# A hybrid decoder layer on one core: where the gate weights are loaded, and which tiles hold a sum of the first stage

## Chip, core and metric

The kernel runs on one core of a Trainium2 chip. The metric is the device time of one execution in microseconds (us), median of several runs.

## The reference

One decoder layer over 1024 tokens of width 1024, in float32. A pre-norm feeds one projection whose columns go to two mixers that run side by side; their outputs are concatenated, projected, added to the input and normed.

```python
xn = rms_norm(h, norm_in_g)
proj = jnp.einsum('btd,de->bte', xn, w_in).astype(f32)
q, k, v, g_ret, x_lru, g_lru = jnp.split(proj, IN_SPLITS, axis=-1)
...
o_ret = group_norm_heads(chunkwise_retention(q, k, v)).reshape(B, T, RET_WIDTH)
y_ret = o_ret * jax.nn.silu(g_ret)
xc = causal_depthwise_conv(x_lru, conv_w.astype(f32), conv_b.astype(f32))
o_lru = rg_lru(xc, gate_a_w.astype(f32), gate_a_b.astype(f32), gate_x_w.astype(f32),
               gate_x_b.astype(f32), lru_lambda.astype(f32))
y_lru = o_lru * jax.nn.silu(g_lru)
mixed = jnp.concatenate([y_ret, y_lru], axis=-1).astype(x.dtype)
h = h + jnp.einsum('bte,ed->btd', mixed, w_out)
return rms_norm(h, norm_out_g)
```

Inside `rg_lru` two block-diagonal products with sigmoids (the gates: 8 blocks of 128x128, two weights each) decide the decay of a linear scan.

## The kernel before

Every operand of a large product is split into a high part (a cast to fp32r on ScalarE, L106) and a low part (the rest, by a subtraction on VectorE, L107); a product is then three matmuls, high by high, high by low and low by high (`mm3`, L112), each of 128x128 weights by 512 columns. Products of two-by-two blocks are made with seven products instead of eight (P1 to P7), from sums and differences of the blocks; the parts of the left sums (of the input x, transposed) are kept for the whole projection.

Stages in the order of time. `v_phase` (L249) computes the column block of v and leaves the left parts behind in their pools sP1 to sP7. Its blocks of x are A11, A12, A21, A22, its blocks of weights b11, b12, b21, b22, and its left sums s1 = A21 - A22, s3 = A11 - A21 (written over A21), s2 = s1 - A11 (written over A11), s4 = A12 + s2. Its products run P1, P2, P5, P6, P7, P3, P4, twelve matmuls for each of four token tiles. The weight blocks and the token tiles whose squares give the norm (`token_rms`, L196, ScalarE L201) share the pool "vb" of six tiles of 4 KB a partition, the outputs have the pool "vo" of ten tiles of 2 KB. Late in the stage b21 is loaded once more for P4.

Then `Runner` (L490) goes through quads of 256 columns: for each of four pairs of blocks one quad of x_lru, one of g_lru, one of g_ret, then eight of q and k. In a quad's step it runs that quad's products with the preparation of the next quad's weights between them (`prep1` to `prep4`; sums t24 and t13 in the pool "sums" of two tiles), and after each product takes one closure from the list `fillers`: this is how the convolution, the gates, the scan and the silu gates of quads done before are put between. After the step of a quad of x_lru, `post_x` (L633) appends fifteen closures: three for the convolution of the first block, `gate_w_parts` (L627), which loads the gate weights of the pair and splits them, and the rest, among them `lru_gates` (L583) for each block. These all work in the pool "w4" of ten tiles of 4 KB ("big", L537); the split gate weights have one tile ("gwp"). After that come retention, whose pieces are fillers in the first half of the output projection, and the rest of the output projection with the norm.

The order of an engine's instructions is set by Tile's scheduler at compile time, which hands out the tiles of a pool and may take an instruction ahead of its place in the program. All loads and stores but one are issued by SP, in its queue's order. In the trace a tile of "sums" is named t, ones or graw, a left sum in its pool xA or xS, and the weight blocks bt.

Of the kernel before, what the change touches and what calls it, by code (L numbers as in the profile page):

```python
# [10 lines left out]
F32 = mybir.dt.float32  # L11
# [3 lines left out]
ALU = mybir.AluOpType  # L15

P = 128
# [23 lines left out]
def hybrid_layer(  # L41
# [17 lines left out]
    pe, act, dve, pool, sp = nc.tensor, nc.scalar, nc.vector, nc.gpsimd, nc.sync  # L59
# [7 lines left out]
    def pool_on(side, name, bufs):  # L67
        return tc.tile_pool(name=name, bufs=bufs, side=side, reuse_waits="tile")
# [36 lines left out]
    def split(src, hi, lo):  # L105
        act.copy(out=hi, in_=src)  # L106
        dve.tensor_tensor(out=lo, in0=src, in1=hi.bitcast(F32), op=ALU.subtract)  # L107
# [57 lines left out]
    sums = s_stack.enter_context(pool_on("right", "sums", 2))  # L165


    xs, xr = {}, {}
# [17 lines left out]
    def combine(out, a, b, op):  # L186
        for o, x_, y_ in zip(out, a, b):
            dve.tensor_tensor(out=o, in0=x_, in1=y_, op=op)  # L188

    def x_parts(name, src):  # L190
        xs[name] = Parts(xs_pool[name])
        for i in range(2):
            xs[name].put(i, src[i])
# [53 lines left out]


    def v_phase():  # L249
        with pool_on("left", "vb", 6) as vb, pool_on("left", "vo", 10) as vo:  # L250
            bw, c, todo = {}, {}, []

            def half():
# [13 lines left out]
            def w_parts(name, src):  # L267
                bw[name] = Parts(slabs)
                for i in range(2):
                    bw[name].put(i, src[i])  # L270
# [48 lines left out]
            s1 = [xs_pool["P3"].tile([P, 2, 512], F32, name="xS1", tag="w") for _ in range(2)]  # L319
# [11 lines left out]

            combine(b11, b11, b22, ALU.add)
            w_parts("P6", b11)
            s3 = xr["A21"]
            combine(s3, xr["A11"], s3, ALU.subtract)
            s2 = xr["A11"]
            combine(s2, s1, s2, ALU.subtract)
            x_parts("P6", s2)
            sp.dma_start(out=cst_sb, in_=cst)
            sp.dma_start(out=ident, in_=ident_in)  # L340
            todo.extend(token_rms(vb, "bt"))
# [36 lines left out]
            decay_exponent()  # L378

    v_phase()  # L380


# [154 lines left out]
    def big(dt=F32, name="big"):  # L537
        return w4.tile([P, T], dt, name=name, tag="w4")


    def post_gr(p):
        def gate(h, c):
            dve.tensor_tensor(out=c, in0=c, in1=rstd_b, op=ALU.mult)
            act.activation(out=c, in_=c, func=AF.Silu)
            sp.dma_start(out=g_d[h // 4, :, :, h % 4].rearrange("n p c -> p n c"),
                         in_=c.rearrange("p (n c) -> p n c", n=NT))

        def post(q):
            for i, c in enumerate((q.cx, q.cy)):
                fillers.append(lambda i=i, c=c: gate(2 * p + i, c))  # L550
        return post
# [4 lines left out]
    def lru_conv(b, c):  # L556

        cw = [col(PAR_CW + 3 * b + j, b) for j in range(CONV)]

        def tap(d):  # L560
            dve.scalar_tensor_tensor(out=xc[:, d:], in0=c[:, :T - d], scalar=cw[3 - d],  # L561
                                     in1=xc[:, d:], op0=ALU.mult, op1=ALU.add)

        def first():
            nonlocal xc
            dve.tensor_tensor(out=c, in0=c, in1=rstd_b, op=ALU.mult)
            xc = big(name="xc")
            act.activation(out=xc, in_=c, func=AF.Identity, scale=cw[3], bias=col(PAR_CB, b))
            tap(1)

        def rest():
            tap(2)
            tap(3)

        def parts():
            xh, xl = big(F32R, "xh"), big(F32R, "xlo")
            split(xc, xh, xl)
            lru[b] = xc, xh, xl

        xc = None  # L580
        return [first, rest, parts]

    def lru_gates(gw, b):  # L583
        xc, xh, xl = lru[b]
        r, y = big(name="r"), big(name="y")
        o = (b % 2) * 256
        for dst, w, bias in ((r, o, PAR_BA), (y, o + P, PAR_BX)):
            for th in range(2):
                s = slice(th * 512, (th + 1) * 512)
                ps = psum()  # L590
                mm3(ps, tuple(gw[:, i, w:w + P] for i in range(2)), (xh[:, s], xl[:, s]), True, True)
                act.activation(out=dst[:, s], in_=ps, func=AF.Sigmoid, bias=col(bias, b))
        dve.tensor_tensor(out=y, in0=y, in1=xc, op=ALU.mult)
        lru[b] = r, y

    def lru_decay(bs):

        for b in bs:
            r, y = lru[b]
            a = big(name="a")  # L600
            act.activation(out=a, in_=r, func=AF.Exp, scale=c1[:, b:b + 1])
            act.activation(out=r, in_=r, func=AF.Exp, scale=c2[:, b:b + 1])
            act.activation(out=r, in_=r, func=AF.Relu, scale=-1.0, bias=1.0)
            lru[b] = r, y, a

    def lru_root(bs):
        for b in bs:
            act.activation(out=lru[b][0], in_=lru[b][0], func=AF.Sqrt)

    def lru_scan(b):  # L610

        r, y, a = lru[b]
        dve.tensor_tensor(out=y, in0=y, in1=r, op=ALU.mult)
        dve.tensor_tensor_scan(out=y, data0=a, data1=y, initial=0.0, op0=ALU.mult, op1=ALU.add)  # L614

    def lru_gated(b, g):
        y = lru.pop(b)[1]
        dve.tensor_tensor(out=y, in0=y, in1=g[b], op=ALU.mult)
        sp.dma_start(out=l_d[b], in_=y)

    def lru_quads():
        quads = []
        for p in range(4):
            bs = (2 * p, 2 * p + 1)
            g, gw = {}, []

            def gate_w_parts(p=p, gw=gw):  # L627
                gr = sums.tile([P, 2, 512], F32, name="graw", tag="sum")
                sp.dma_start(out=gr[:, 0], in_=gate_w[:, 512 * p:512 * p + 512])
                gw.append(gwp.tile([P, 2, 512], F32R, name="gw", tag="gw"))  # L630
                split(gr[:, 0], gw[0][:, 0], gw[0][:, 1])

            def post_x(q, bs=bs, gw=gw, gate_w_parts=gate_w_parts):  # L633
                x0, x1 = lru_conv(bs[0], q.cx), lru_conv(bs[1], q.cy)
                fillers.extend(x0 + [
                    gate_w_parts, x1[0], lambda: lru_gates(gw[0], bs[0]), *x1[1:], None, None,
                    lambda: lru_gates(gw[0], bs[1]), lambda: lru_decay(bs), lambda: lru_root(bs), lambda: lru_scan(bs[0]),
                    lambda: lru_scan(bs[1])])

            def post_g(q, bs=bs, g=g):  # L640
                def gate(b, c):
                    dve.tensor_tensor(out=c, in0=c, in1=rstd_b, op=ALU.mult)
                    act.activation(out=c, in_=c, func=AF.Silu)
                    g[b] = c
                for b, c in zip(bs, (q.cx, q.cy)):
                    fillers.extend([lambda b=b, c=c: gate(b, c), lambda b=b: lru_gated(b, g)])

            quads.append(Quad(C_XL + 256 * p, w4, "w4", post_x))
            quads.append(Quad(C_GL + 256 * p, w4, "w4", post_g))
            quads.append(Quad(C_G + 256 * p, w4, "w4", post_gr(p)))  # L650
        return quads
# [497 lines left out]
```

## Time and profile before

| | us |
|---|---|
| median of 3 runs (748.37 to 748.61) | 748.6 |
| the profiled execution | 748.8 |
| its span, first to last instruction | 747.0 |
| TensorE busy (PE) | 724.4 |
| VectorE busy (DVE) | 582.7 |
| ScalarE busy (ACT) | 425.5 |

Times in the views are microseconds from the start of the span. In a timeline row stand the start, the duration, the engine, the line of the code, the operation, what it writes and reads, the count of like instructions merged into the row, and in brackets the idle time of the engine before it with what ended it. SPq and PEld are SP's queue of transfers and TensorE's loading of weights. The ends of matmuls are modelled and overlap; their starts are what counts.

### The profile page before, as it was taken

The page shows a single profiled execution, that of the slowest core. Times are in us where ns is not written, and L with a number is a line of the kernel's source. Part 1 is how long each engine was busy: PE and PEld are TensorE (multiplying, and loading weights), DVE is VectorE, ACT ScalarE, POOL GpSimd, SP SyncE. Part 2 cuts the span into 40 slices and gives each one's busy share as a digit, 9 for nine tenths or more (in the row PEclk, how much of TensorE's full clock was granted, in tenths as well). Part 3 has the DMA queues.
Part 4 walks back from the last instruction along what each step waited for, and adds up shares of the span by engine and source line. Part 5 has one row for each costly group of instructions (what it writes and reads, how often), then busy time and mean ns, then how long its engine had stood idle before and what let it go on. Part 6 is the DMA issues. An engine that isn't in the chain of part 4 may idle for free.

```text
span 747.0 us, 9358 instructions
## 1 busy us (share of the span) xinstructions
PE 724.4 (97%) x3448; PEld 601.7 (81%) x3448; DVE 582.7 (78%) x960; ACT 425.5 (57%) x649; POOL 0.2 (0%) x4
## 2 busy tenths in 40 slices
PE   6999999999999999999999999997999999999995
PEld 5877888887788788878788888886989988888884
DVE  6899647678977977996799988686467565779996
ACT  6795435695689679669833333244444445424545
POOL 0000000000000000000000000000000000000000
PEclk9999999999999999999999999999899999999998
DMA  9862712122213410421644444569897776272006
GB/s 308 279 207 86 254 56 72 57 84 85 70 57 105 135 57 32 142 97 54 197 126 128 114 113 113 141 187 286 273 312 255 253 210 211 72 228 81 1 0 226
DMA packets 93806, 107.68 MB, mean 144 GB/s; under 512 B 4928, under 2 KB 66752, under 8 KB 93760
## 3 DMA queue, kind: packets, MB, share of 16 engines
q1 hardware_dynamic: 93616, 106.82, 45.5%
q8 instruction: 27, 0.44, 0.2%
q10 hardware_dynamic: 144, 0.26, 0.1%
q14 instruction: 19, 0.16, 0.1%
HBM read 77.71 MB, written 29.36 MB: 143 GB/s over the span
## 4 chain that ended last, share of the span: by engine, by line
PE 55%; DVE 22%; ACT 11%; DMA 7%; issue 4%; SPq 0%; DVEq 0%; ACTq 0%
PE pp L112 47%; DVE xc L561 2%; DVE h L1003 2%; PE pp L796 2%; PE pp L835 2%; PE pp L834 2%; DVE wt L107 2%; PE pp L817 1%; DVE wq L107 1%; DVE y L614 1%; PE pp L856 1%; ACT wq L106 1%; DVE blk L188 1%; DMA rot<-in_rot_t 1%; DMA blk<-o_d 1%
## 5 line engine op out<-in xcount | busy, mean ns | idle before, releaser
L112 PE MATMUL pp<-wh,wq 128*128 128x512 f32 x960 | 301.5, 390 | 1.6 <-DVE cy L471 0.7
L112 PEld LDWEIGHTS pp<-wh,wq 128*128 128x128 f32 x960 | 179.9, 188 | 42.5 <-ACT cy L461 2.3
L112 PE MATMUL pp<-wl,wq 128*128 128x512 f32 x480 | 186.9, 389 | 0.0
L112 PEld LDWEIGHTS pp<-wl,wq 128*128 128x128 f32 x480 | 90.1, 188 | 18.6
L112 PE MATMUL pp<-wo,yt 128*128 128x512 f32 x384 | 98.4, 403 | 0.0
L112 PEld LDWEIGHTS pp<-wo,yt 128*128 128x128 f32 x384 | 70.7, 191 | 13.1
L107 DVE TENSOR_TENSOR wq<-t,wq 128x1024 fp32r<-128x1024 f32 x40 | 48.6, 1220 | 38.6 <-ACT wq L106 31.5
L106 ACT CAST wq<-t 128x1024 fp32r<-128x1024 f32 x40 | 41.7, 1051 | 31.7 <-PE pp L112 22.0
L112 PE MATMUL pp<-wh,w 128*128 128x512 f32 x160 | 52.9, 391 | 0.1
L112 PE MATMUL pp<-wh 128*128 128x512 f32 x112 | 45.5, 406 | 6.9 <-ACT wh L106 6.9
L112 PE MATMUL pp<-wl,wh 128*128 128x512 f32 x112 | 44.6, 400 | 0.0
L112 PE MATMUL pp<-wh,wl 128*128 128x512 f32 x112 | 44.2, 399 | 0.0
L112 PEld LDWEIGHTS pp<-wh,w 128*128 128x128 f32 x160 | 30.0, 188 | 6.9 <-DVE w L107 0.6
L461 ACT COPY cy<-pp 128x512 f32<-128x512 f32 x20 | 11.6, 581 | 41.9 <-PE pp L112 41.3
L848 ACT ACTIVATE yn<-pp,nb,rs_y 128x128 f32<-128x128 f32 x64 | 24.1, 457 | 17.2 <-DVE nb L846 17.2
L112 PEld LDWEIGHTS pp<-wh 128*128 128x128 f32 x112 | 21.7, 194 | 12.1 <-ACT wh L106 7.3
L112 PE MATMUL pp<-wl,w 128*128 128x512 f32 x80 | 31.1, 389 | 0.0
L112 PE MATMUL pp<-wt,ylh 128*128 128x512 f32 x96 | 29.6, 389 | 0.0
L112 PE MATMUL pp<-wt,qkch 128*128 128x512 f32 x96 | 29.6, 389 | 0.0
L422 ACT CAST wq<-wraw 128x512 fp32r<-128x512 f32 x40 | 22.9, 617 | 9.0 <-PE pp L112 8.2
L106 ACT CAST wt<-blk 128x1024 fp32r<-128x1024 f32 x14 | 14.6, 1050 | 21.5 <-PE pp L112 18.0
L424 DVE TENSOR_TENSOR wq<-wraw,wq 128x512 fp32r<-128x512 f32 x40 | 26.8, 681 | 0.1
(179 smaller groups left out, 1303.7 us busy)
## 6 DMA issues: line engine op xcount, KB each, us to landing
wraw<-in_w_in SPq DMA_DIRECT2D x40, 512.0 KB, 4.8
qkc<-qk_d SPq DMA_DIRECT2D x16, 512.0 KB, 6.3
blk<-in_w_out SPq DMA_DIRECT2D x12, 512.0 KB, 5.5
bt<-in_w_in SPq DMA_DIRECT2D x20, 256.0 KB, 5.4
xA<-in_xT SPq DMA_DIRECT2D x16, 256.0 KB, 5.4
v_d<-vo SPq DMA_DIRECT2D x16, 256.0 KB, 2.3
xt<-in_x SPq DMA_DIRECT2D x8, 512.0 KB, 3.3
l_d<-y SPq DMA_DIRECT2D x8, 512.0 KB, 3.0
```

The costliest lines, as they stand in the source:

```text
L106: act.copy(out=hi, in_=src)
L107: dve.tensor_tensor(out=lo, in0=src, in1=hi.bitcast(F32), op=ALU.subtract)
L112: pe.matmul(ps, a, b, start=first and j == 0, stop=last and j == 2, skip_group_check=True)
L422: act.copy(out=h[:, j], in_=b)
L424: dve.tensor_tensor(out=l[:, j], in0=b, in1=h[:, j].bitcast(F32), op=ALU.subtract)
L461: act.copy(out=self.cy[:, :TH], in_=self.A)
L561: dve.scalar_tensor_tensor(out=xc[:, d:], in0=c[:, :T - d], scalar=cw[3 - d], in1=xc[:, d:], op0=ALU.mult, op1=ALU.add)
L796: heads(lambda h, hs: pe.matmul(psc[:, hs], k[:, hs], q[:, hs], start=True, stop=True))
L834: pe.matmul(po[:, hs], q[:, hs], st[:, h], start=True, stop=False)
L835: pe.matmul(po[:, hs], sm[:, h], vn[:, hs], start=st is None, stop=True)
L848: heads(lambda h, hs: act.activation(out=yn[:, hs], in_=po[:, hs], func=AF.Identity, scale=rs[:, h:h + 1], bias=nb[:, h:h + 1]))
L1003: last_add[0] = dve.tensor_tensor(out=r, in0=r, in1=ps, op=op_)
```

## The change

The pool "vb" has seven tiles, "vo" eight (as many bytes as before). s2 is written into two new tiles of "vb" instead of over A11, and it and its parts come before s3 in the program. The gate weights are loaded by a closure of their own, `gate_w_load`, that `post_x` calls at once instead of leaving it to the fourth closure (which still splits them), into a tile of "w4" instead of one of "sums".

```diff
-        with pool_on("left", "vb", 6) as vb, pool_on("left", "vo", 10) as vo:
+        with pool_on("left", "vb", 7) as vb, pool_on("left", "vo", 8) as vo:
...
             w_parts("P6", b11)
+            s2 = [vb.tile([P, 2, 512], F32, name="xS2", tag="bt") for _ in range(2)]
+            combine(s2, s1, xr["A11"], ALU.subtract)
+            x_parts("P6", s2)
             s3 = xr["A21"]
             combine(s3, xr["A11"], s3, ALU.subtract)
-            s2 = xr["A11"]
-            combine(s2, s1, s2, ALU.subtract)
-            x_parts("P6", s2)
...
-            def gate_w_parts(p=p, gw=gw):
-                gr = sums.tile([P, 2, 512], F32, name="graw", tag="sum")
-                sp.dma_start(out=gr[:, 0], in_=gate_w[:, 512 * p:512 * p + 512])
+            def gate_w_load(p=p, gw=gw):
+                gw.append(big(name="gr"))
+                sp.dma_start(out=gw[0][:, :512], in_=gate_w[:, 512 * p:512 * p + 512])
+
+            def gate_w_parts(gw=gw):
+                gr = gw.pop()
                 gw.append(gwp.tile([P, 2, 512], F32R, name="gw", tag="gw"))
-                split(gr[:, 0], gw[0][:, 0], gw[0][:, 1])
+                split(gr[:, :512], gw[0][:, 0], gw[0][:, 1])
...
+            def post_x(q, bs=bs, gw=gw, gate_w_load=gate_w_load, gate_w_parts=gate_w_parts):
+                gate_w_load()
```

## Rows read from the trace of the kernel before

**Rows 1.** The page, first part: busy time of each engine, share of the span, instructions.

```profile
PE 724.4 (97%) x3448; PEld 601.7 (81%) x3448; DVE 582.7 (78%) x960; ACT 425.5 (57%) x649; POOL 0.2 (0%) x4
```

**Rows 2.** TensorE's waits: tile and line, releaser, us in total, times, longest.

```profile
PE pp L112 <- ACT wh L106: 6.9, 2, 6.2
PE pp L796 <- DMA qkc<-qk_d: 4.0, 1, 4.0
PE pp L112 <- ACT gw L106: 1.9, 3, 1.0
```

**Rows 3.** Timeline of TensorE around the end of P5 and the start of P6.

```profile
41.59 0.39 PE L112 MATMUL pp<-wl,wh 128*128 128x512 f32 x1
41.81 0.39 PE L112 MATMUL pp<-wh,wl 128*128 128x512 f32 x1
42.88 0.50 PE L112 MATMUL pp<-wh 128*128 128x512 f32 x1 [0.68 <-ACT wh L106]
...
44.62 0.40 PE L112 MATMUL pp<-wl,wh 128*128 128x512 f32 x1
45.03 0.50 PE L112 MATMUL pp<-wh,wl 128*128 128x512 f32 x1
```

**Rows 4.** Timelines of VectorE and, last row, ScalarE, in P5 and P6.

```profile
35.82 1.22 DVE L188 TENSOR_TENSOR xA<-xA,xA 128x1024 f32<-128x1024 f32 x1
...
40.36 2.35 DVE L188 TENSOR_TENSOR xA<-xS,xA 128x1024 f32<-128x1024 f32 x2
...
49.44 1.22 DVE L107 TENSOR_TENSOR wl<-bt,wh 128x1024 fp32r<-128x1024 f32 x1
...
41.80 1.03 ACT L106 CAST wh<-xA 128x1024 fp32r<-128x1024 f32 x1
```

**Rows 5.** Timelines of SP's queue, VectorE and ScalarE around the second gate load.

```profile
192.01 0.35 SPq L629 DMA_DIRECT2D graw<-in_gate_w  x1
...
189.02 1.23 DVE L107 TENSOR_TENSOR xlo<-xc,xh 128x1024 fp32r<-128x1024 f32 x1
...
190.77 1.22 DVE L107 TENSOR_TENSOR wq<-t,wq 128x1024 fp32r<-128x1024 f32 x1
...
196.72 0.62 ACT L106 CAST gw<-graw 128x512 fp32r<-128x512 f32 x1 [1.81 <-DMA graw<-in_gate_w]
```

**Rows 6.** Timeline of TensorE where it comes to the gates.

```profile
195.99 0.39 PE L112 MATMUL pp<-wl,wq 128*128 128x512 f32 x1
197.39 0.50 PE L112 MATMUL pp<-xh,gw 128*128 128x512 f32 x1 [1.02 <-ACT gw L106]
...
260.81 0.50 PE L112 MATMUL pp<-xh,gw 128*128 128x512 f32 x1 [0.28 <-ACT gw L106]
...
321.60 0.61 PE L112 MATMUL pp<-wh,wq 128*128 128x512 f32 x2
322.79 0.50 PE L112 MATMUL pp<-xh,gw 128*128 128x512 f32 x1 [0.57 <-ACT gw L106]
```

**Rows 7.** Timeline of VectorE: last reader, and next writer, of a tile of "sums".

```profile
178.32 1.22 DVE L107 TENSOR_TENSOR wq<-t,wq 128x1024 fp32r<-128x1024 f32 x1
...
181.79 0.68 DVE L415 TENSOR_TENSOR t<-wraw 128x512 f32<-128x512 f32 x1
```

**Rows 8.** The token tiles (min/median/max), loads of weight blocks, and TensorE at P4.

```profile
L200 SPq DMA_DIRECT2D xt<-in_x x8: 327/328/384, 28.5 to 47.8; - x8
L201 ACT ACTIVATE xt<-xt x8: 1053/1062/1071, 31.9 to 51.7; 128x1024 f32<-128x1024 f32 x8
...
DMA to landing us min/median/max: 3.3/3.3/4.7
...
bt<-in_w_in SPq DMA_DIRECT2D x20, 256.0 KB, 5.4
...
73.94 0.79 PE L112 MATMUL pp<-wh 128*128 128x512 f32 x1
```

**Rows 9.** Timeline of TensorE, a wait of another kind among the quads.

```profile
370.28 0.50 PE L112 MATMUL pp<-wh,wq 128*128 128x512 f32 x1 [0.74 <-DVE cy L471]
```

More of the change, by code (lines that the diff above doesn't have):

```diff
@@ L625, in lru_quads @@
             g, gw = {}, []
-            def gate_w_parts(p=p, gw=gw):
-                gr = sums.tile([P, 2, 512], F32, name="graw", tag="sum")
-                sp.dma_start(out=gr[:, 0], in_=gate_w[:, 512 * p:512 * p + 512])
+            def gate_w_load(p=p, gw=gw):
[3 more added lines that the diff above has]
+                gr = gw.pop()
                 gw.append(gwp.tile([P, 2, 512], F32R, name="gw", tag="gw"))
-                split(gr[:, 0], gw[0][:, 0], gw[0][:, 1])
-            def post_x(q, bs=bs, gw=gw, gate_w_parts=gate_w_parts):
+                split(gr[:, :512], gw[0][:, 0], gw[0][:, 1])
+            def post_x(q, bs=bs, gw=gw, gate_w_load=gate_w_load, gate_w_parts=gate_w_parts):
+                gate_w_load()
                 x0, x1 = lru_conv(bs[0], q.cx), lru_conv(bs[1], q.cy)
```

## The prediction

> **What bounds the kernel now.** I read the engine sums first: TensorE is busy 724.4 of a span of 747.0 us [rows 1]. The kernel is one long stream of matmuls, and only what makes TensorE wait can be won. Next the list of TensorE's waits [rows 2]: three entries carry nearly all of them. 6.9 us is for casts on ScalarE (6.2 us of it the start of the program, before there is anything to multiply), 4.0 us is one load at the start of the retention stage, and 1.9 us, in three waits, is for the cast of the gate weights. The change aims at the rest of the first entry and at the whole third. The profiled execution took 748.8 us, 0.2 above the median of 748.6; about 1.8 us lie outside its span.
>
> What a wait costs I take from the starts of the matmuls. In undisturbed stretches one of 512 columns starts every 0.227 us (41.59 and 41.81 are such a pair [rows 3]); what a start-to-start distance has above that is lost.
>
> **First part: the second left sum in tiles of its own.** Before the product P6, VectorE makes four operations that use A11: two for s3 and two for s2, which overwrites A11 and must therefore come last. In the trace s3 starts at 35.82 and s2 only at 40.36; s2's first half is cast on ScalarE at 41.80 [rows 4], and TensorE, which started P5's last matmul at 41.81, starts P6 at 42.88 [rows 3]. That is 1.07 - 0.23 = 0.84 us, and another 0.41 - 0.23 = 0.18 us between 44.62 and 45.03, where the low part of the same half is late: 1.02 us in all. With s2 in new tiles nothing forces s3 ahead of it. Two additions of about 1.14 us each (two took 2.35 in a row [rows 4]) move behind, so s2's two halves can be done 2.3 us earlier, at about 40.4 instead of 42.7; the casts follow 1 us later, ahead of the need. Removed: 1.02 us. No arithmetic is added. s3 becomes 2.3 us later; it is needed by the next product, P7, which starts 48 matmuls (10.9 us) after P6, so P6 itself hides it. What is late next at P6 is the low part of its weights; it is made between s3 and s2 today, so it too is there before TensorE comes to P6.
>
> The two tiles are paid by the output tiles (ten become eight). Twelve outputs and then four more pass through these; by program order the ninth needs what the first has left, three products earlier, so I cost it at nothing; the cover is those products, some 30 us, against a landing of a few us. And the eight squares of the token sums use the same seven tiles as s2: b11, b12 and s2 hold six of them, so between s2 and the end of P7 they run through one tile instead of two. That is the change's real price and it is a rival below.
>
> **Second part: the gate weights.** In the trace the load of the gate weights stands on SP's queue until 192.01, and starts 0.02 us after the operation at 190.77 (1.22 us) that last reads a tile of the pool "sums" [rows 5]. It lands, ScalarE casts at 196.72 after 1.81 us of waiting for it, and TensorE starts the gate matmul at 197.39 [rows 5, 6]. The gate's other operand was done long before: its low part was made at 189.02 plus 1.23 [rows 5]. So the load is late because of its tile, and nothing else of the gate is. One thing tells how tiles are handed out: one of the two "sums" tiles was let go by the operation that ends at 179.5, and the load, which depends on nothing else, didn't take it; the sum at 181.79, ahead of it in the program, did [rows 7]. Tiles of a pool go in program order.
>
> The three waits cost, start to start: 1.40 - 0.23 = 1.17 us at 197.39; at 260.81 the idle time shown is 0.28, and by the first wait, where 1.02 shown are 1.17 lost, I count 0.44; at 322.79 a record is missing behind the pair at 321.60 (the low-part matmul that ends each group of three), which would have started at 322.05, so 0.74 - 0.23 = 0.51 [rows 6]. The fourth piece, the first in time, has no wait. Sum: 2.12 us.
>
> In the changed kernel the load takes one of the ten working tiles at the end of the quad before and needs no "sums" tile. By the program some five of the working tiles are in use at that time (two columns of each of the two quads in hand, one convolved channel), and about eight half a quad earlier, while the scans of the pair before still run; so a tile is free, and the load, 0.35 us of SP's time [rows 5], is issued at the latest with its quad, some ten us before its cast now waits. The cast (0.62 us [rows 5]) and the subtraction are the same instructions, earlier, in time that is idle now; the peak of ten tiles comes after gate_w_parts has released the eleventh. "sums" now serves the weight sums alone, whose allocations were interleaved with the load's: a gain that can't be seen on TensorE here, costed at nothing. Of what SP is moved past: the load now goes ahead of the next pair of weight loads and behind one store; its own 0.35 us is nothing, its wait for a tile could hold the pair, which at that time waits for its own tile anyway.
>
> **Sum.** 1.02 + 2.12 = 3.1 us. From the profiled 748.8 that gives 745.7; from the median, 745.5 us. Bounds of this: the first part gives 0 to 1.02, the second 1.7 (if the smallest wait stays) to 2.12; beyond that a new order of the instructions may take or give one wait of the kind seen at 370.28, 0.74 us idle for an evacuation [rows 9], once or twice. So 743.8 to 747.0.
>
> **Rivals.** *The time comes back as waits for evacuations.* The gate matmuls go forward some 7 us, and with them a table load and four sigmoids on ScalarE, which also evacuates the products. Between P6 and P7 of a quad lies one product of 12 matmuls, 2.7 us, as cover. Each of the three gates may now run into an evacuation; I take the 0.74 us of 370.28 for each [rows 9]: 3 x 0.74 = 2.2 us, leaving 748.6 - 3.1 + 2.2 = 747.7. For it: this wait exists in the trace. Against: the gates run beside evacuations today too, and none of TensorE's three large entries is of this kind [rows 2].
>
> *The squares run out of tiles (slower).* Place: the last products of the first stage, 50 to 76 us. One square's round through a tile is 3.3 us from issue to landing and 1.06 of work: 4.4 us [rows 8]. Eight in one tile are 35 us. The reload of b21 stands behind them in program order; today the last square's load is issued at 47.8, the reload after it, and P4 needs it at 73.94 [rows 8]. From the issue to the finished parts I count 5.4 for landing (the median of these loads [rows 8]), then an addition, a cast and a low part, 1.2, 1.0 and 1.2 [rows 4]: about 9 us, so it may be issued as late as 65 without cost. If the squares start at 28.5 as now, one tile alone would end them at 63.4: just in time. If they must wait until s2 has its tiles (36), they end at 70.9 and P4 starts 6 us late: 745.5 + 6 = 751.5. The point from which this makes the kernel slower than before is a reload after 68. Against it: b12's two tiles come free when its low parts are done, the second at 49.44 + 1.22 [rows 4], and then three tiles serve the squares; by that count the last ends at about 56 to 60, and nothing is late. ScalarE takes its instructions in order in this trace, so a late square also holds the casts behind it: a wait of that kind is the 1.81 us at 196.72 [rows 5]. The Trainium skill, "TensorE: Matmul & The Clock Gate", section "Architectural detail: the array is 16x 32x32, not 1x 128x128", says that ScalarE's queue is strictly first in, first out, where TensorE may pull weight loads ahead; it speaks against the change, since a square without its load would block the casts of P7. By that rule alone, eight such waits would be 14.5 us of ScalarE; the profile shows ScalarE busy for 57% of the span [rows 1], so there is idle time to take them, and I don't add it to the sum.
>
> *It does only half.* The gate matmuls keep their place because the order is set by something else, and only the first stage gains: 748.6 - 1.0 = 747.6.
>
> **How the numbers follow.** Forecast 0.63, evacuations 0.18, only half 0.08, squares 0.11. Predicted: 745.5 us. What a measurement of this kernel can tell from no change is about 0.2%, 1.5 us: 747.1 and below is faster, 750.1 and above slower. The forecast's range is faster; of the two rivals near 747.6 a little is too: faster 0.66, same 0.23, slower 0.11. The range reaches from 743.8 (two evacuation waits go as well) over the forecast and the two rivals at 747.6 and 747.7 with half a wait more, 748.2; out of it are the squares and the edges.
>
> **What would show it.** Right: in the list of TensorE's waits the entry for the gate weights is gone and the one for casts is 6.2 to 6.3; P6 follows P5 after 0.23 us; the gate load is issued ten or more us before its cast, with no wait for "sums". Wrong: new entries of ScalarE evacuations near the gates; a wait between 60 and 76 us with the reload of b21 issued after 65; or the stall of 4.0 us for the retention load, which I take to move along unchanged, grown or doubled. If the load waits for a working tile, SP's own list of waits will name it.

## The result, and the profile after

The changed kernel takes 742.8 us (median of six runs, 740.2 to 744.4) against 748.5 of the kernel before in runs on the same chip: ratio 0.9928, 95% interval 0.9901 to 0.9955, that is 3.4 to 7.4 us faster. The forecast was 745.5 with a range of 743.8 to 748.2: the sign is right, the gain is larger than forecast, and the time lies below the range. The profiled execution took 741.5 us, 739.7 of it the span.

First the engine sums and the list of TensorE's waits, as in [rows 1, 2] (tile and line, releaser, us in total, times, longest).

```profile
PE 720.5 (97%) x3448; PEld 600.8 (81%) x3448; DVE 583.1 (79%) x960; ACT 425.6 (58%) x649; POOL 0.2 (0%) x4
```

```profile
PE pp L112 <- ACT wh L106: 5.8, 1, 5.8
PE pp L800 <- DMA qkc<-qk_d: 3.7, 1, 3.7
PE pp L112 <- DVE cy L471: 1.2, 1, 1.2
PE pp L112 <- ACT cy L461: 0.6, 2, 0.5
...
```

TensorE has as many instructions as before; the entry for the gate weights is gone, the one for casts is left with the start of the program alone, and the stall of the retention load has moved along unchanged (4.0 before, 3.7 now; 3.1 and 5.2 in the second profiles of the two kernels). The wait for VectorE's evacuation, 0.74 in [rows 9], has grown to 1.2.

The end of P5 and the starts of P6 and P7, to be read against [rows 3]: P5's last matmul starts at 40.42, P6's first at 40.64, P7's first at 51.52.

```profile
40.42 0.39 PE L112 MATMUL pp<-wh,wl 128*128 128x512 f32 x1
40.64 0.39 PE L112 MATMUL pp<-wh 128*128 128x512 f32 x1
...
51.52 0.39 PE L112 MATMUL pp<-wh 128*128 128x512 f32 x1
```

In the kernel before, the matmul behind P6's first and the first of P7 are these:

```profile
43.22 0.40 PE L112 MATMUL pp<-wl,wh 128*128 128x512 f32 x1
...
54.24 0.39 PE L112 MATMUL pp<-wh 128*128 128x512 f32 x1
```

The reason, on VectorE and ScalarE, against [rows 4]. The two halves of s2 (xS<-xS,xA) are made at 34.75 and 38.16, each is cast as soon as it ends, and s3 (xA<-xA,xA) comes behind them, at 40.43 and 42.70.

```profile
34.75 1.22 DVE L188 TENSOR_TENSOR xS<-xS,xA 128x1024 f32<-128x1024 f32 x1
...
38.16 1.21 DVE L188 TENSOR_TENSOR xS<-xS,xA 128x1024 f32<-128x1024 f32 x1
...
40.43 1.22 DVE L188 TENSOR_TENSOR xA<-xA,xA 128x1024 f32<-128x1024 f32 x1
...
36.00 1.05 ACT L106 CAST wh<-xS 128x1024 fp32r<-128x1024 f32 x1
39.40 1.05 ACT L106 CAST wh<-xS 128x1024 fp32r<-128x1024 f32 x1 [2.35 <-DVE xS L188]
```

The gate loads on SP's queue, and TensorE where it comes to the second gate, against [rows 5, 6]. The load of the second piece is issued at 166.43 in place of 192.01, 22 us before TensorE wants it, and the gate follows the matmul before it after 0.23 us; so it does at 252.31 and 314.98.

```profile
166.43 0.58 SPq L629 DMA_DIRECT2D gr<-in_gate_w  x1
...
188.56 0.39 PE L112 MATMUL pp<-wh,wq 128*128 128x512 f32 x1
188.79 0.39 PE L112 MATMUL pp<-xh,gw 128*128 128x512 f32 x1
...
314.98 0.39 PE L112 MATMUL pp<-xh,gw 128*128 128x512 f32 x1
```

What is late now: one low part in the first stage, and one evacuation among the quads; and, against [rows 8], the token loads and squares, the reload of b21 and P4.

```profile
64.60 0.50 PE L112 MATMUL pp<-wh,wl 128*128 128x512 f32 x1 [0.22 <-DVE wl L107]
...
365.52 0.50 PE L112 MATMUL pp<-wh,wq 128*128 128x512 f32 x1 [1.17 <-DVE cy L471]
...
73.80 0.39 PE L112 MATMUL pp<-wh 128*128 128x512 f32 x1
```

```profile
L201 ACT ACTIVATE xt<-xt x8: 1053/1066/1078, 40.4 to 60.6; 128x1024 f32<-128x1024 f32 x8
```

```profile
58.92 1.40 SPq L262 DMA_DIRECT2D bt<-in_w_in  x3
```

The last square starts at 60.6 instead of 51.7, the reload goes out at 56 to 60, and P4 starts at 73.80 without a wait. In the kernel before, the row at 73.94 in [rows 8] isn't P4's first: it stands behind the four matmuls of the diagonal (72.60), and with it 15 matmuls of P3 are still to come. Counted at 48 matmuls a product, P4 starts there at 77.79. In the changed kernel the diagonal comes inside P4, at 76.45, so not all of the 4 us between 77.79 and 73.80 are a gain.

### The profile page after: what moved, and what is told of

Same layout as the page of the kernel before. It is cut to its first block, busy times and chain, and to the rows that moved or that the text cites. A ratio compares the mean times of both kernels' runs of the same rounds, so it can differ in the third digit from the quotient of the medians.

```text
span 739.7 us, 9358 instructions
## 1 busy us (share of the span) xinstructions
PE 720.5 (97%) x3448; PEld 600.8 (81%) x3448; DVE 583.1 (79%) x960; ACT 425.6 (58%) x649; POOL 0.2 (0%) x4
## 4 chain that ended last, share of the span: by engine, by line
PE 79%; ACT 8%; DVE 5%; DMA 4%; issue 2%; SPq 1%; DVEq 0%; ACTq 0%
PE pp L112 71%; PE pp L839 2%; PE pp L800 2%; PE pp L838 2%; PE pp L821 1%; PE pp L860 1%; DMA rot<-in_rot_t 1%; DMA qkc<-qk_d 1%; DMA vc<-v_d 1%; DMA xt<-in_x 1%; PE pp L807 1%; ACT wq L106 1%; DVE y L614 1%; ACT L601 1%; ACT wh L106 0%
```

## The experiments

Two figures are worked out alike from the TensorE timeline of every kernel: the time from P5's last matmul to P7's first (48 matmuls of P6, 11.1 us if nothing waits), and the sum of what the start-to-start distances between 100 and 380 us, where the gates lie, have above 0.2268 us, the undisturbed distance to one digit more. The ratio given for a run isn't the quotient of the two medians, and differs from it by up to 0.0017; gains in us, with their intervals, are taken from the ratio. The table is the yield of all runs; the rows behind it follow.

| kernel | to the kernel before, 95% | idle at P6, us | P5's last to P7's first, us | lost from 100 to 380, us |
|---|---|---|---|---|
| before | | 0.68 | 12.43 | 7.8 |
| before again | 0.9979 to 1.0025 | 2.28 | 15.14 | 7.9 |
| first part alone | 0.9955 to 1.0000 | 0 | 11.11 | 7.7 |
| second part alone | 0.9924 to 0.9968 | 1.70 | 13.27 | 4.2 |
| changed | 0.9901 to 0.9955 | 0 | 11.10 | 5.0 |
| changed again | 0.9889 to 0.9948 | 0 | 11.11 | 4.9 |
| its tile alone | 0.9970 to 1.0003 | 0.70 | 12.45 | 6.0 |
| its place alone | 0.9948 to 0.9976 | 2.42 | 15.44 | 4.0 |
| squares later | 0.9985 to 1.0011 | 0.59 | 12.43 | 8.5 |
| no squares | 0.9976 to 1.0000 | 0.84 | 12.77 | 7.3 |
| changed, eight tiles | 0.9893 to 0.9937 | 0 | 11.10 | 4.6 |
| changed, load kept in "sums" | 0.9912 to 0.9939 | 0 | 11.11 | 4.1 |
| that, retention moved by 12 matmuls | 0.9873 to 0.9913 | 0 | 11.10 | 4.4 |
| changed, retention moved by 24 | 0.9985 to 1.0019 | 0 | 11.10 | 4.6 |

**Both kernels once more.** No edit.

> The kernel before once more, unchanged: it shows by how much single executions and single profiles of one program differ. Forecast theory (the change is worth its waits, 3.1 us, and the other 2.3 us of the measured 5.4 are the spread between executions): this profile's span differs from the first one of before (747.0) by 2 us or more, and the difference lies where the granted clock is low (start, the wait for qkc at the start of the retention, the end), not among the quads. Rival (the change also shortens the retention and the end by its new order): this profile has the same low-clock stretches as the first, within 0.5 us each, and its landmarks stand within 0.5 us of the first ones.

> The changed kernel once more. Spread theory: ratio to before near 0.995 (3 to 4 us), single executions over a range of 4 us or more, the stretch from the first gate to the last quad product as in the first profile within 0.3 us, the stretches at the start and at the retention's first wait different by a us or more. Order theory: 5 to 6 us faster again, with the same landmarks.

Measured: the kernel before 748.17 us (ratio 1.0002), the changed one 743.28 (0.9918, a gain of 6.1 us, 3.9 to 8.3). The gain stands; that it is 3 to 4 us and the rest spread, as the spread theory had it, isn't borne out. But the second profile of the kernel before isn't the first: TensorE idles 2.28 us at P6 where [rows 3] show 0.68, and starts again slowly. TensorE, then VectorE and ScalarE, then the windows (us, PE busy, granted clock, DMA share, GB/s):

```profile
41.31 0.39 PE L112 MATMUL pp<-wh,wl 128*128 128x512 f32 x1
43.98 0.80 PE L112 MATMUL pp<-wh 128*128 128x512 f32 x1 [2.28 <-ACT wh L106]
44.57 0.63 PE L112 MATMUL pp<-wl,wh 128*128 128x512 f32 x1
45.00 0.63 PE L112 MATMUL pp<-wh 128*128 128x512 f32 x1
```

```profile
40.63 2.35 DVE L188 TENSOR_TENSOR xA<-xS,xA 128x1024 f32<-128x1024 f32 x2
...
41.84 1.06 ACT L201 ACTIVATE xt<-xt 128x1024 f32<-128x1024 f32 x1 [0.38 <-DMA xt<-in_x]
42.80 0.19 ACT L201 ACTIVATION_READ_ACCUMULATOR xt<-xt 128x1 f32 x1
42.90 1.03 ACT L106 CAST wh<-xA 128x1024 fp32r<-128x1024 f32 x1
```

```profile
44.00:46.00 2.00, 2.00 (x5) 0.50 0.81 260
```

VectorE has the first half of s2 at 41.85 (its two operations start at 40.63), but on ScalarE the square of a token tile stands ahead of the cast, starts at 41.84 when its load has landed, and holds the cast to 42.90: 1.05 of the 2.28 us are the square's. The token loads landed later here; the row of line 200, to be read against [rows 8]:

```profile
DMA to landing us min/median/max: 3.1/3.5/5.3
```

So the wait that the first part removes isn't one size: in the five profiles with s2 over A11 and the squares at their old place it is 0.68, 0.70, 1.70, 2.28 and 2.42 us. In each of the three long ones a square holds the cast, by 1.05 to 1.24 us past the end of VectorE's first half; in the short ones by 0.22 and 0.25. In two of the long ones an earlier square also holds a cast for which VectorE waits, 0.34 and 0.35 us. With the second part alone (1.70 us) that first half is done at 41.64:

```profile
41.83 1.06 ACT L201 ACTIVATE xt<-xt 128x1024 f32<-128x1024 f32 x1 [1.54 <-DMA xt<-in_x]
...
42.88 1.03 ACT L106 CAST wh<-xA 128x1024 fp32r<-128x1024 f32 x1
```

**One part at a time.** The first part alone has the hunks of v_phase only; the second alone those of the gates only.

> The first part alone (second left sum in its own tiles, vb 7, vo 8). Forecast theory: P6 follows P5 without a gap (1.0 us less), the wait at 64.6 us (0.4) and the later rstd product that the changed kernel shows come with it, so 0.3 to 1.0 us faster, 747.5 to 748.2; the three waits for the gate weights are there as before. Order theory: more than 1.5 us faster, with the surplus after 500 us.

> The second part alone (gate weights loaded early into the phase's pool). Forecast theory: the three waits go, 2.1 us, 746.4; P6's wait of 0.84 us stays. Order theory: 4 us or more faster, 744.5 or below, with the surplus after 500 us.

Measured: 746.09 us and 744.23 us, 1.6 us (0 to 3.4) and 4.0 us (2.4 to 5.7) faster. Their sum, 5.6, is what both bring together, so neither hides the other. Each brings more than its term in the forecast, 1.0 and 2.1. In the table each part moves its own column and leaves the other alone. So do the waits, the first line from the first part alone, the second from the second part alone (with the 1.7 us of P6 in it):

```profile
PE pp L112 <- ACT gw L106: 1.6, 3, 0.9
```

```profile
PE pp L112 <- ACT wh L106: 8.0, 2, 6.3
```

The order theory put what is more than forecast behind 500 us. It isn't there: from the last weight product to the end these two profiles take 244.9 and 244.5 us, the second one of the kernel before 244.5.

**Which half of the second part pays.** Its tile alone: the load stays in gate_w_parts and takes a working tile.

```
+            def gate_w_load(p=p, gw=gw):
+                gw.append(big(name="gr"))
...
+            def gate_w_parts(gw=gw, gate_w_load=gate_w_load):
+                gate_w_load()
+                gr = gw.pop()
```

> The kernel before, with one thing altered: the gate weights are loaded into a working tile and not into a tile of "sums"; the load stays at its old place in the program, with its cast. Theory (the tile held the load): the load goes out well ahead of 192 us in the second piece, ScalarE's cast no longer waits 1.81 us for it, the entry for the gate weights (1.9 us in three waits) leaves the list of TensorE's waits, and the time falls by about as much as with the whole second part, 744.5 to 746.0 us (2.2 to 3.7 faster). Rival (the place in the program is what pays): the load goes out where it did, the entry stays above 1.2 us, and the time is 747.3 or more.

Its place alone: the load is called at the head of post_x, but from "sums".

```
+            def gate_w_load(p=p, gw=gw):
+                gw.append(sums.tile([P, T], F32, name="graw", tag="sum"))
...
+                gate_w_load()
                 x0, x1 = lru_conv(bs[0], q.cx), lru_conv(bs[1], q.cy)
```

> The kernel before, with the other half of the second part: the load is called at the end of the quad before, as in the changed kernel, but its tile still comes from "sums". Theory (the tile held the load): called earlier it takes the "sums" tile that came free at 179.5, keeps it until its own cast, and the two weight sums then share one tile; the gate waits may go, but VectorE's sums and the low parts behind them come late, and waits on wq or wl take their place: 747.5 to 750.5 us. Rival (the place is what pays): no gate entry, no new entry, 744.5 to 746.0 us.

Measured: 747.14 us for the tile alone (1.0 us faster, -0.2 to 2.2), 744.99 for the place alone (2.8 us, 1.8 to 3.9). My theory falls: the place pays, the tile alone gives less (the two intervals overlap; the last column of the table, 6.0 and 4.0 against 7.8, agrees). The rival for the tile alone, that the load would go out where it did, isn't met either. The gate loads on SP's queue, and the gate that still waits, with the tile alone:

```profile
117.95 0.50 SPq L629 DMA_DIRECT2D gr<-in_gate_w  x1
177.57 1.20 SPq L629 DMA_DIRECT2D gr<-in_gate_w  x1
242.43 0.98 SPq L629 DMA_DIRECT2D gr<-in_gate_w  x1
314.44 0.45 SPq L629 DMA_DIRECT2D gr<-in_gate_w  x1
```

```profile
319.82 0.50 PE L112 MATMUL pp<-xh,gw 128*128 128x512 f32 x1 [0.70 <-ACT gw L106]
```

With the place alone:

```profile
178.52 0.35 SPq L629 DMA_DIRECT2D graw<-in_gate_w  x1
237.07 0.34 SPq L629 DMA_DIRECT2D graw<-in_gate_w  x1
300.29 0.34 SPq L629 DMA_DIRECT2D graw<-in_gate_w  x1
```

The tile takes the load from 192.01 to 177.57 in the second piece and from 257.02 to 242.43 in the third, but in the last one only from 318.84 in the kernel before to 314.44, too late by 0.70 us. The place brings all of them forward by 13 to 20 us, and the tile that the load then gets is one of "sums" that is handed out earlier. It costs little here: near 291 to 296 us the weight sums come late and TensorE loses 1.3 us in short waits, the longest shown 0.21.

**The squares.** In the kernel before, token_rms is appended behind P6's loop:

```
-            todo.extend(token_rms(vb, "bt"))
             for t in range(4):
                 product("P6", A[t], t, False, False)
                 snap("c12", t, A[t])
-                fill()
+            todo.extend(token_rms(vb, "bt"))
```

> The kernel before, with the squares of the token tiles put behind P6 in the program; s2 is still written over A11, after s3. Theory (the wait at P6 varies because a square, waiting for its load, stands ahead of the cast of s2 in ScalarE's order): no square lies before that cast, the cast starts when VectorE has the first half of s2, about 41.5, the idle time at P6 is 0.5 us or less against 0.68 to 2.3 in the runs of the kernel before, no stretch of lower clock follows P6, and the time falls by 1 to 2 us, to 746.2 to 747.2. Rival (the order on VectorE sets the wait, and its size comes from elsewhere): idle time at P6 of 0.7 us or more, 748 us. The squares run later, up to about 70 us; if the token sums then come late, TensorE waits at the matmuls of the diagonal by some us and the time is over 749.

Measured: 747.17 us, ratio 0.9998. The run doesn't tell the theories apart: the schedule of the engines still puts four squares early, and one of them ahead of the cast.

```profile
40.13 1.06 ACT L201 ACTIVATE xt<-xt 128x1024 f32<-128x1024 f32 x1 [0.43 <-DMA xt<-in_x]
...
41.19 2.09 ACT L106 CAST wh<-xA 128x1024 fp32r<-128x1024 f32 x2
```

It shows one thing: the token sums may come 8 us later (the diagonal's matmuls at 80.9 in place of 72.6) without harm. So the squares were taken out, with the eight token loads that feed them; a constant takes the place of the sums, so this kernel leaves the normalisation out:

```
-                xt = pl.tile([P, T], F32, name="xt", tag=tag)
-                sp.dma_start(out=xt, in_=x[t * P:(t + 1) * P, :])
-                act.activation(out=xt, in_=xt, func=AF.Square, accum_out=ss[:, t:t + 1])
+                dve.memset(ss[:, t:t + 1], 1.0)
```

> The kernel before without the squares of the token tiles and their eight loads (the sums of squares are a constant, so the normalisation is left out); s2 is still written over A11 after s3. Six profiles of kernels with s2 over A11 show an idle time at P6 of 0.6 to 0.7 us or of 1.7 to 2.4 us, the long one where a token load landed 1.1 to 1.4 us later and its square stands ahead of the cast of s2. Theory (the order on VectorE gives only the small part, the square ahead of the cast the rest): the cast starts when VectorE has the first half, about 41.5, the idle time at P6 is 0.3 to 0.5 us, no row of lower clock follows, and the time is 746.0 to 747.2 us. Rival (something other than the squares makes the long wait): idle time of 0.65 us or more, 747.5 us or more.

Measured: 746.64 us, 0.9 us faster (0 to 1.8). ScalarE now casts when VectorE is done (40.06 plus 1.23), and TensorE still idles 0.84 us:

```profile
41.33 1.04 ACT L106 CAST wh<-xA 128x1024 fp32r<-128x1024 f32 x1 [3.43 <-DVE xA L188]
```

```profile
42.42 0.50 PE L112 MATMUL pp<-wh 128*128 128x512 f32 x1 [0.84 <-ACT wh L106]
```

The time is as the theory wanted, the wait is twice what it said. So VectorE's order by itself is worth about 0.8 us here, the whole of the short form of the wait. That the squares make the long form is read from the three profiles above; one execution without them can't show that it is gone for good, and since the loads went with the squares, the run doesn't tell the two apart.

**More tiles for the squares.** In the changed kernel the pools are vb 8 and vo 6 in place of 7 and 8.

> The changed kernel with the same bytes dealt out otherwise: eight block tiles and six output tiles where it has seven and eight, so that the squares have two tiles while s2 lives. Theory (the squares' shortage of tiles costs nearly nothing in the changed kernel): all that can go is the idle time of 0.38 us near 64.6, so 0 to 0.5 us faster than the changed kernel, 742.4 to 743.2. Rival (the late squares still cost through ScalarE's order): over 1 us faster, 742.0 or less. The other way, six output tiles are too few: VectorE's or ScalarE's outputs wait for their stores, a new wait for evacuations appears between 50 and 75 us, and the time is 744 or more.

Measured: 741.95 us, ratio 0.9915 against 0.9918 and 0.9928 of the changed kernel: no difference clear of the intervals, though 741.95 us taken by itself would be the rival's number. The wait near 64.6 isn't gone, it is 0.49 at 63.81. So the shortage of tiles didn't make it.

**The load of the retention.** In the changed kernel two empty slots, that is 24 matmuls of the output product, are put behind the second piece of the retention:

```
-    fillers.extend([None, None, p_a, None, p_b] + rest)
+    fillers.extend([None, None, p_a, None, p_b, None, None] + rest)
```

> The changed kernel with 24 matmuls of the output product put between the first state of the retention and the scores of its second half, for whose load TensorE waits 3.7 to 5.2 us in every profile so far. Theory (this wait, and the lower clock in which TensorE comes out of it, set how far two executions of one kernel lie apart): the entry for this load leaves the list of TensorE's waits, the granted clock from 510 to 530 us stays at 0.9 or more, the stretch from the last weight matmul to the end falls from 244.2 to 247.1 us to about 239.5, and the time is 736.5 to 739 us. Rival (the retention has no slack, what is moved comes back at its end or as another wait): 741.5 us or more, with the new wait after 600 us.

Measured: 748.11 us, 1.0002: all that the change had gained is lost, as the rival had it. The wait for the load is gone and the granted clock from 510 to 530 us is 1.00, but waits for the normalised outputs take its place, at 616 and 660 us, where the retention ends. There the clock falls instead: 0.93 in the mean from 600 to 625 us and 0.89 from 650 to 680, where the changed kernel has 1.00 in both.

```profile
PE pp L860 <- ACT yn L852: 7.3, 4, 4.3
...
```

**The gate load early, but in "sums", with s2 in its own tiles.**

> The changed kernel, but the gate weights, still loaded three pieces ahead, keep their tile of "sums". Theory (it is the place in the program that pays, the pool adds little): within 1 us of the changed kernel, 742.0 to 743.8 us, no gate entry in TensorE's waits. Rival (the two weight sums need both tiles of "sums"): waits for wq and the weights of about 1.3 us as near 290 us in the kernel with the early load alone, in more than one quad, and 744.5 us or more.

Measured: 742.03 us, 0.9925, within what the theory gave, and no gate entry among the waits: beside the place, the pool adds nothing that can be measured. The same kernel with one empty slot (12 matmuls) behind the retention's second piece:

> The kernel with the early gate load in "sums" and s2 in its own tiles, with 12 matmuls of the output product (2.7 us) put between the first state of the retention and the scores of its second half, where 24 brought back 7.3 us as waits for the normalised outputs at 616 and 660 us. Theory (the end of the retention has some slack, less than 24 matmuls): the wait for the load falls from 3.4 us to 0.7 or less, the waits for the normalised outputs together are 2 us or less, and the time is 740.0 to 741.5 us against 742.0. Rival (no slack at all): what the load gives back comes again at the end of the retention, 742 us or more.

Measured: 739.19 us (738.7 to 741.8), ratio 0.9893, 0.9873 to 0.9913: the lowest ratio of this study, 2.4 us below the same without the slot. The two ran on different chips and their intervals just touch, so this step is likely, not settled; in the profiles the stretch from the last weight product to the end falls from 244.7 to 241.4 us. The time is below the forecast of 740.0 to 741.5. Its waits:

```profile
PE pp L112 <- ACT wh L106: 6.2, 1, 6.2
PE pp L860 <- ACT yn L852: 2.2, 1, 2.2
PE pp L112 <- ACT cy L461: 0.8, 1, 0.8
PE pp L112 <- DVE wq L424: 0.2, 1, 0.2
PE pp L800 <- DMA qkc<-qk_d: 0.2, 1, 0.2
```

The stall of 3.4 us is 0.2, and the wait for the outputs grows from 0.8 to 2.2, a little over the 2 expected; the low clock behind the stall goes as well. The windows from 510 to 530 us (PE busy, granted clock, DMA share, GB/s) of the kernel before, the changed one and this one:

```profile
510.00:530.00 20.00, 16.03 (x77) 0.83 1.01 302
```

```profile
510.00:530.00 20.00, 16.25 (x96) 0.91 0.92 294
```

```profile
510.00:530.00 20.00, 19.81 (x122) 1.00 0.92 295
```

## Why the prediction was right in its sign and wrong in its size

**The mechanism** is the one forecast: P6 follows P5 after 0.23 us, the gates have no wait, and each part moves its own place alone. **Two terms of the sum were mis-sized.**

*The first part, 1.02 us.* Two errors. The smaller: a wait costs more than the distance up to the matmul that waited. In [rows 3] that matmul is 0.50 long and not 0.39, and the next one, at 43.22, starts 0.34 behind it and not 0.23; the same again behind 45.03. From P5's last matmul to P7's first the profile of before has 12.43 us (41.81 to 54.24) where 11.10 are needed: 1.33. The larger: I took one execution for the kernel. In the five profiles with s2 over A11 and the squares at their old place the excess is 1.33, 1.35, 2.17, 4.04 and 4.34 us, on average 2.65; the profile I had shows the smallest. In its place stands a new loss of 0.4 us on average in P3, as at 64.60 (seven profiles with s2 in its own tiles). What is left, 2.2 us, agrees with the 1.6 (0 to 3.4) measured for this part alone.

The sentence that failed with it is the one on ScalarE, in the rival of the squares. I had the fact that it takes its instructions in order, and counted it only against the change, for the casts of P7. The Trainium skill, "TensorE: Matmul & The Clock Gate", section "Architectural detail: the array is 16x 32x32, not 1x 128x128", which calls ScalarE's queue strictly first in, first out, agrees with the rows: the square that begins at 41.84 holds a cast whose input is there at 41.85. But it holds the cast of P6 in the kernel before, and so it speaks for the change.

*The second part, 2.12 us.* I assumed that a record was missing ahead of 322.79 and took 0.23 off. The profiles of the kernel before and the changed one have the same 960 and 480 records of this product, and the five profiles with the late load show 0.66 to 0.74 us there; nothing is missing. With the 0.11 behind each wait, here too, and the low parts that come late in the same way, the three waits and the fourth piece cost 3.0 us in that same profile. The mean is 7.8 us lost from 100 to 380 with the late load (five profiles) and 4.7 with both halves of the part (five): 3.2 us, against 4.0 (2.4 to 5.7) measured.

So the sum is 2.2 + 3.2 = 5.4 us, where 5.7 and 4.9 lie between the medians and the ratios give 5.4 and 6.1. From the profile I had, read without the two errors of counting, it would have been 1.33 + 3.0 = 4.3, and 744.3 us: inside my range. The rest could not be read from one execution; a range with its low end at 743.8 treated the waits as constants. (Its ends are also 0.1 to 0.2 wider than what they are worked out from: two waits of 0.74 off 745.5 leave 744.0, half a wait on 747.7 gives 748.1. The measured time lies outside either way.)

**"The load is late because of its tile, and nothing else"** is half wrong. The tile alone moves the load too little for one gate in three; the place alone does all of it, with the old pool. What I had read from [rows 7], that tiles of a pool go in program order, agrees with that: called earlier, the load gets an earlier tile.

**Costed at nothing.** The output tiles, eight in place of ten, and even six, cost nothing that can be measured. s3's later place is hidden by P6 as forecast: P7 follows P6 without a gap. SP's queue holds the gate load twice for a working tile, up to 3.0 us; nobody waits for that.

**The rivals.** The evacuations came back by 0.6 us (1.2 and 0.6 us in the list against 0.74 [rows 9] and 0.5), not by 2.2. The squares run a little later than counted in their harmless form (an end at 56 to 60): the last starts at 60.6, the reload goes out at 56 to 60. The harmful form was overpriced: it took 73.94 for the start of P4, which is at 77.79, so parts ready at about 80 would have come some 2 us late and not 6. *Only half* is excluded by the two runs of one part each.

**The profiled pair** differs by 7.3 us, more than the medians, because 2.5 us of it belong to neither part: from the last weight product to the end of the span the kernel before takes 246.7 us and the changed one 244.2, but in the second profiles it is 244.5 and 247.1, the other way round. These are two forms of the stretch behind the retention's stall.

## What to carry to other kernels

One profile gives one sample of every wait that ends with a DMA; before a wait is put into a sum, see what stands ahead of its releaser on that engine's queue, and whether a load decides when that is done. Count a stall up to where the stream is regular again, not up to the first matmul. And when a load is late, try its place in the program before its memory; when a stall is moved away from its load, move it by no more than the end of that chain has slack.

## What the runs showed of the hardware that was not expected

After idling 2.28 us at P6 TensorE came back at the 1.2 GHz level: granted clock 0.50 from 44 to 46 us, and the next seven matmuls start 0.59 and then 0.41 to 0.43 us apart instead of 0.23, 1.5 us more on top of the wait. After 2.42 us, in the kernel with the place alone, it did so too: from 44.37 on its matmuls start 0.43 apart. After 1.70 us in the kernel with the second part alone it did not.

At the retention's stall it does so in every profile that has the stall, in two sizes: from 510 to 530 us the mean granted clock is 0.91 in nine profiles and 0.83 in three (the kernel before, the changed one's second profile, and the one without squares), and 1.00 in the two where the stall is moved away. The stretch to the end is about 2.5 us longer in the first two of the three than in the others of the same kernel. Whether an execution gets the one or the other, the runs don't say; that this makes up much of the spread of 2 to 7 us among executions of one kernel is argued, not shown.
